# Neighbourhood attention with query tiles shifted by half a key tile, joined context heads, and modulation blocks summed in one op

## The chip, the core and the metric
The kernel runs on one core of a Trainium2 chip. Five engines work from queues of their own: TensorE (PE: matmuls and transposes, with weight loads shown apart as PEld), VectorE (DVE), ScalarE (ACT), GpSimd (POOL) and SyncE (SP), which issues all DMA transfers here. The metric is the device time of one execution in microseconds, as a median of several runs.

## What is computed
One inference step of a backbone of four layers on 128 context tokens and 512 latent tokens (a grid of 8 rows and 64 columns), all in float32. Cut to what matters here:

```
for l in range(4):                      # kind: 0 global, 1 window, 2 neighbourhood, 0 global
    shift, scale, gate = split(silu(c) @ w_mod[l] + b_mod[l])     # for latent and for context
    u = rms_norm(h, norm_pre[l]) * (1 + scale) + shift
    q, k, v, z = split(u @ w_in[l])     # 1024, 256, 256, 1024 columns; q, k get RMSNorm per head
    kind 0, 1: rotary positions on q and k
    latent tokens attend to: kind 0 all latent keys; kind 1 latent keys within +-128;
        kind 2 all 8 rows x a clamped window of 16 columns, with a relative bias per head;
        and always to 128 cached context keys, in one softmax (kind 1 with a sink logit)
    context tokens attend to context tokens only
    h = h + gate * rms_norm((o * silu(z)) @ w_out[l], norm_post[l])
return h_ctx, h_lat, new_cache_k, new_cache_v
```
There are 16 query heads of 64 columns in 4 groups that share keys and values.

## The kernel before
**Order of work.** All instructions are first put down as ops with their reads, writes and buffers (`S.op`, L92). A planner (`emit`, L130) then walks a modelled time and takes, again and again, the op that can start first; ties and look-ahead go by a number for each op, its place in the program plus an offset for the part of the kernel it belongs to (`ORDER`, L29; `MODSHIFT`, `SSHIFT`, `WINDOW`). What it issues on an engine stays in that order on the chip. Buffers are pools with a fixed number of slots (`CAPS` and L227): an op that needs a free slot can't be planned before there is one.

**Precision.** Projections and scores are made of float32r matmuls on a high and a low part of each operand: a copy on ScalarE makes the high part, a subtraction on VectorE (or GpSimd) the low one (`split`, L263). Raw weights come in by tiles of 128x512 (256 KB) into buffers named raw, of which there are six, and are split into buffers named w, of which there are eight (`start_w`, L322).

**A layer.** `kv_chunk` (L561) projects keys and values of five token tiles of 128 (tile 0 is the context). Then, twice, for half of the heads: `q_chunk` (L601) projects, normalizes, rotates and transposes the queries of five tiles into five buffers q, `z_block` (L632) makes the gate, and `lat_pair` (L748) does latent attention for four pairs of heads: scores (L702 for global layers, L728 for the two band layers), the addition of mask or bias with a running maximum (L731), exponential (L741), scaling by the reciprocal sum (L662), transposes of the probabilities (L777) with their eviction (L260), the product with the values (L784) and the product with the gate (L791). `ctx_heads` (L795) does the same for the context's queries in groups of four heads (L804, L830, L838, L843). At the end of a layer `split_og` splits the gated output, and `out_phase` (L910) multiplies by w_out and makes the next layer's input (L455 to L467).

**Layer 2.** Here tokens are ordered by blocks of 16 grid columns, so a key tile is 8 rows x 16 columns and query tiles are the same blocks. A query tile needs its own block and its neighbours, and the context tile (number 4): `BAND` (L45) lists 3, 4, 4 and 3 key tiles for the four query tiles, `UNION` the key tiles of a pair of query tiles, `BATCHES` how their transposes go into PSUM banks (four banks for each half of a pair of heads, with 4, 4, 3 and 3 transposes). `bias_tiles` (L666) builds, for each head, two tiles of bias plus mask on GpSimd from a strided load of the bias table: two clears and four additions, which wait for the last query buffer (L754). The token order is changed in layer 1's last stage (`rows`, L488, and `split_og`), and changed back at the end of layer 2.

**Modulation.** The vector silu(c) for latent and context is multiplied by w_mod in blocks of 512 output columns, as four concurrent column strips of TensorE. A block is two ops of four k each (`mod_half`, L371), which add into one PSUM bank that is held from the first to the second; a half takes four raw buffers, and `cap_raw` lets modulation have no more than four. `mods` (L477) hands out the 40 halves over the phases of the layers by the table `MODS` (L21), so that they fall between other work.

Of the kernel before, what the change touches and what calls it, by code (L numbers as in the profile page):

```python
# [20 lines left out]
MODS = [[1, 3, 3, 3, 2, 0, 0], [1, 3, 3, 3, 2, 0, 0], [1, 3, 3, 3, 2, 0, 0], [1, 2, 1, 0, 0, 0, 0]]  # L21
# [4 lines left out]
           (([(0, (0, 2))], [(1, (0, 2))], [(0, (2, 4))], [(1, (2, 4))]),))  # L26


ORDER = {'mf': -51, 'tab': 230, 'kv': 673, 'ks': -1156, 'nat': 29, 'hn': -564, 'mod': 211, 'w': -2, 'qt': 6,  # L29
         'z': 99, 'sc': 231, 'st': -343, 'pv': -1242, 'cx': 15, 'og': 10, 'out': -36, 'no': 283, 'un': -775,  # L30
         'up': -335, 'bt': -16, '': -11}
MODSHIFT = -121
SSHIFT = -248
WINDOW = 257
# [3 lines left out]
SLACK = {'P': 89, 'V': 0, 'A': 234, 'G': 0, 'D': 521}  # L38
DISLIKE = {'V2': 0, 'V': 933, 'Ap': 365, 'G': 1080, 'mad': 968, 'mada': 3985, 'G1': 612}
CAPS = {'p': 6, 'raw': 6, 'cap_prep': 3}  # L40
# [4 lines left out]
BAND = {0: [0, 1, 4], 1: [0, 1, 4, 2], 2: [1, 2, 4, 3], 3: [4, 2, 3]}  # L45
TILES = ((0, 1), (2, 3, 4))
UNION = {0: [0, 1, 4, 2], 1: [2, 3, 4, 1]}
# [14 lines left out]
class Sched:  # L62
# [17 lines left out]
    def __init__(self, nc):  # L80
        self.nc = nc
        self.eng = {"P": nc.tensor, "V": nc.vector, "A": nc.scalar, "G": nc.gpsimd, "D": nc.sync}
        self.tags, self.ops, self.shift, self.part = {}, [], 0, ""
        self.prev, self.line = [], {}
# [7 lines left out]
    def op(self, alts, r=(), w=(), touch=(), seq=None):  # L92
# [25 lines left out]
        self.ops.append((alts, deps, list(bufs.values()), i + self.shift + ORDER.get(self.part, 0)))  # L118
# [94 lines left out]
def build(ctx, tc, a, o):  # L213
# [61 lines left out]
    identr = persist("identr", [128, 128], F32R)  # L275
    mhalf = persist("mhalf", [128, 1])
    S.op([("G", 1500, lambda e: make_identity(nc, ident.ap), "id")], w=[ident])
    S.op([V2(128, lambda e: e.tensor_copy(identr.ap, ident.ap))], r=[ident], w=[identr])
# [57 lines left out]
    def mod_part(l, b, mod, tag):  # L336
# [15 lines left out]
        S.op([P(935, mm, "E")], r=raws + [cpad], w=[ps], touch=[cap])  # L352
# [18 lines left out]
    def mod_half(l, s, mod, half, st):  # L371
# [7 lines left out]
        for kk, raw in enumerate(raws):  # L379
            S.op([D(256, lambda e, raw=raw, kk=kk: e.dma_start(raw.ap, a["w_mod"][l, s, 4 * half + kk]))], w=[raw],  # L380
                 touch=[caps[kk]])

        def mm(e):
            for kk in range(4):
                k = 4 * half + kk
                for g in range(4):
                    e.matmul(ps.ap[32 * g:32 * g + 32, 0:128], cpad.ap[:, k, :], raws[kk].ap[:, 128 * g:128 * g + 128],  # L387
                             start=k == 0, stop=k == 7, skip_group_check=True)
# [88 lines left out]
    def mods(l, phase, i, n):  # L477
# [3 lines left out]
        for _ in range(m * (i + 1) // n - m * i // n):  # L481
            if queue:
                mod_half(*queue.pop(0))
# [4 lines left out]
    def rows(t, perm, tau):  # L488
        if tau == 0:
            return t[0:128]  # L490
        if perm:
            return t[128:640].rearrange("(r j c) d -> j r c d", r=8, j=4)[tau - 1]
        return t[128 * tau:128 * tau + 128]
# [107 lines left out]
    def q_chunk(l, tabs, c):  # L601
        W = load_w(a["w_in"], l, c)
        Q = []
        for tau in range(5):
            ps, pcap = S.buf("B", [128, 512]), S.buf("cap_proj")
            q = S.buf("q", [128, 8, 128], F32R)
            nat(lambda ps=ps: ps.ap, ps, [pcap], tau, W, [q])
# [13 lines left out]
            for x in range(2):  # L621
                hi, lo = (slice(0, 64), slice(64, 128))[::1 - 2 * x]
                d = lambda rows, x=x, q=q: q.ap.rearrange("p (r x) t -> p x r t", x=2)[rows, x]
                v = lambda hi=hi, pt=pt: pt.ap[hi].rearrange("p (r t) -> p r t", r=4)
                S.op([As(512, lambda e, d=d, v=v, hi=hi: e.activation(d(hi), v(), AF.Copy))], r=[pt], w=[(q, x)], touch=[cap])
                S.op([V(512, lambda e, d=d, v=v, hi=hi, lo=lo: e.tensor_sub(d(lo), v(), d(hi).bitcast(F32)))], r=[pt, (q, x)],  # L626
                     w=[(q, x)], touch=[cap])
            Q.append(q)
# [37 lines left out]
    def bias_tiles(l, h, tabs, after):  # L666
        tab = tabs["tab"]
        raw = lambda: tab.ap[:, 896 + 265 * (h % 2):1161 + 265 * (h % 2)]
        S.op([D(300, lambda e: e.dma_start(raw(), bass.AP(tensor=a["na"].tensor, offset=a["na"].offset + 512 * h,
                                                         ap=[[31, 8], [1, 16], [1, 265]])))], w=[(tab, h % 2)])  # L670

        def rel(a0, n):
            x = raw()
            return bass.AP(tensor=x.tensor, offset=x.offset + 264 - 16 * a0,
                           ap=[list(x.ap[0]), [-16, n], [-31, 8], [-1, 16]])

        b03, b12 = tmp([128, 640]), tmp([128, 512])
        v = lambda x: x.rearrange("p (a r c) -> p a r c", r=8, c=16)
        S.op([G1(128, lambda e: e.memset(b03.ap[:, 256:384], 0.0))], r=after, w=[(b03, 256)])
        S.op([G1(128, lambda e: e.memset(b12.ap[:, 256:384], 0.0))], r=after, w=[(b12, 256)])  # L680
# [398 lines left out]
```

## Time and profile before
| | |
|---|---|
| median of 3 runs | 1366.44 us (1366.27 to 1368.22) |
| the profiled execution | 1366.54 us, of which the span from first to last instruction is 1364.8 us |
| TensorE matmul busy | 1331.3 us (98% of the span) |
| TensorE weight loads busy | 1097.1 us (80%) |
| VectorE, ScalarE, GpSimd busy | 971.9, 753.5 and 212.9 us (71, 55 and 16%) |
| DMA | 145.61 MB, 107 GB/s in the mean |

Busy time of an engine is the union of its instructions. Matmuls are pipelined, so one record is longer than the distance to the next start; what a matmul costs is read from the distances of starts. In a timeline a merged row gives the start of its first instruction, the time to the end of its last, and the count; the distance to the next row's start is what the group took of the engine.

### The profile page before, as it was taken

What the parts mean: (1) busy time and instruction counts of PE and PEld (TensorE: products, weight loads), DVE (VectorE), ACT (ScalarE), POOL (GpSimd) and SP (SyncE); (2) the same over time, 40 slices, a digit from 0 to 9 for tenths busy, and PEclk for the clock granted to TensorE, in tenths of its full rate; (3) what the DMA queues carried; (4) which work ended last, traced back from release to release, by engine and by line L of the source; (5) the groups of instructions that cost most, each with busy time, mean ns of one, the idle gap of its engine ahead of it and who ended that gap; (6) DMA issues with size and microseconds to landing.
All of it is one profiled execution on the core that took longest, in us unless ns stands there. A gap on an engine that the chain in (4) does not pass through costs nothing.

```text
span 1364.8 us, 24827 instructions
## 1 busy us (share of the span) xinstructions
PE 1331.3 (98%) x9208; PEld 1097.1 (80%) x9208; DVE 971.9 (71%) x2298; ACT 753.5 (55%) x1823; POOL 212.9 (16%) x231
## 2 busy tenths in 40 slices
PE   6999999999999999999999999999999999999998
PEld 3778888888877888788878888788777888888876
DVE  4878667766597866876487678678579776586753
ACT  4545663666353675477355368358445366547741
POOL 1320002000142100100032441342023300020000
PEclk9999999999999999999999999999999999999999
DMA  8532222304333423332644343242534220110042
GB/s 339 172 107 80 78 93 81 106 32 161 135 121 96 137 79 93 104 98 72 184 133 135 120 122 102 70 122 67 163 130 155 91 95 1 63 62 1 30 133 101
DMA packets 76521, 145.61 MB, mean 107 GB/s; under 512 B 12976, under 2 KB 17136, under 8 KB 76400
## 3 DMA queue, kind: packets, MB, share of 16 engines
q1 hardware_dynamic: 76400, 144.02, 32.5%
q8 instruction: 73, 1.20, 0.4%
q14 instruction: 48, 0.39, 0.1%
HBM read 132.42 MB, written 11.57 MB: 106 GB/s over the span
## 4 chain that ended last, share of the span: by engine, by line
PE 80%; DVE 13%; issue 3%; ACT 2%; POOL 1%; DMA 1%; SPq 0%; DVEq 0%; POOLq 0%; ACTq 0%
PE B L501 16%; PE B L638 13%; PE B L777 9%; PE B L784 9%; PE S L905 8%; PE B L905 6%; PE S L702 5%; PE S L728 4%; PE B L387 2%; DVE q L626 2%; DVE tmp L467 1%; POOL sm L311 1%; DVE w L266 1%; PE S L501 1%; PE B L618 1%
## 5 line engine op out<-in xcount | busy, mean ns | idle before, releaser
L311 POOL TENSOR_TENSOR sm<-sm,mhalf 128x1 f32<-128x1 f32 (+2 forms) x100 | 130.3, 1305 | 667.6 <-DVE sm L306 352.5
L260 ACT ACTIVATE pt<-B 128x512 f32<-128x512 f32 (+1 forms) x300 | 161.2, 575 | 101.8 <-PE B L777 91.7
L501 PE MATMUL B<-w,uB 128*128 128x512 f32 x816 | 201.3, 399 | 0.0
L501 PEld LDWEIGHTS B<-w,uB 128*128 128x128 f32 x816 | 150.0, 188 | 33.4 <-issue 0.2
L638 PE MATMUL B<-uB,w 128*128 128x384 f32 x768 | 164.6, 345 | 0.0
L777 PE MATMUL B<-ident,p 128*128 128x128 f32 x1088 | 155.1, 277 | 2.1 <-ACT pt L260 0.8
L266 DVE TENSOR_TENSOR w<-raw,w 128x512 fp32r<-128x512 f32 x212 | 141.7, 698 | 5.7 <-ACT w L265 5.2
L777 PEld LDWEIGHTS B<-ident,p 128*128 128x128 f32 x1088 | 122.5, 140 | 24.0 <-issue 8.8
L501 PE MATMUL B<-w,uA 128*128 128x512 f32 x528 | 136.9, 403 | 0.8 <-DVE tmp L467 0.7
L705 DVE TENSOR_REDUCE sm<-S 128x1 f32<-128x640 f32 x128 | 103.5, 821 | 47.6 <-PE S L702 46.7
L265 ACT ACTIVATE w<-raw 128x512 fp32r<-128x512 f32 x224 | 131.7, 626 | 6.6 <-PE B L638 2.8
L784 PE MATMUL B<-pt,vt 128*64 128x256 f32 (+1 forms) x1152 | 131.6, 373 | 0.0
L638 PEld LDWEIGHTS B<-uB,w 128*128 128x128 f32 x768 | 128.6, 189 | 1.5 <-issue 0.7
L662 DVE TENSOR_SCALAR p<-p,sm 128x640 f32<-128x640 f32 (+2 forms) x244 | 123.7, 519 | 6.8
L707 ACT ACTIVATE p<-S,sm 128x640 f32<-128x640 f32 x128 | 101.8, 797 | 42.3 <-DVE sm L705 32.8
L638 PE MATMUL B<-uA,w 128*128 128x256 f32 x768 | 114.7, 286 | 0.1
L501 PEld LDWEIGHTS B<-w,uA 128*128 128x128 f32 x528 | 95.1, 188 | 23.0 <-issue 2.6
L784 PEld LDWEIGHTS B<-pt,vt 128*64 128x64 f32 x1152 | 77.0, 136 | 45.2 <-issue 8.0
L638 PEld LDWEIGHTS B<-uA,w 128*128 128x128 f32 x768 | 102.3, 189 | 2.4 <-issue 0.8
L702 PE MATMUL S<-kst,q 128*128 128x320 f32 x512 | 100.5, 324 | 1.1 <-ACT p L707 0.8
L741 ACT ACTIVATE p<-p,sm 128x512 f32<-128x512 f32 (+1 forms) x128 | 84.0, 658 | 12.0 <-DVE sm L739 11.8
L510 ACT ACTIVATE tmp<-B 128x512 f32<-128x512 f32 (+1 forms) x56 | 30.1, 537 | 106.0 <-PE B L501 82.6
(141 smaller groups left out, 2049.6 us busy)
## 6 DMA issues: line engine op xcount, KB each, us to landing
raw<-in_w_in SPq DMA_DIRECT2D x160, 256.0 KB
raw<-in_w_mod SPq DMA_DIRECT2D x160, 256.0 KB
raw<-in_w_out SPq DMA_DIRECT2D x64, 256.0 KB
w<-in_w_first SPq DMA_DIRECT2D x16, 512.0 KB
xs<-q SPq DMA_DIRECT2D x15, 512.0 KB
q<-xs SPq DMA_DIRECT2D x15, 512.0 KB
q<-in_x SPq DMA_DIRECT2D x10, 512.0 KB
kst<-gs SPq DMA_DIRECT2D x8, 512.0 KB
```

Of the source, the lines that this page charges most:

```text
L260: alts = {"A": Ap(n, lambda e: e.activation(out(), in_(), AF.Copy)), "V": V(n, lambda e: e.tensor_copy(out(), in_()))}
L265: S.op([As(n, lambda e: e.activation(h(), src(), AF.Copy))], r, w)
L266: f = lambda e: e.tensor_sub(l(), src(), h().bitcast(F32))
L311: S.op([("G", 395 + 157 * n, lambda e: e.tensor_tensor(r.ap, v.ap, mhalf.ap.to_broadcast([128, n]), op=OP.pow), "pow")], r=[v, mhalf], w=[r])
L501: e.matmul(ps(), t.ap[:, s, k, off:off + 128], W[k].ap[:, w], start=k == 0 and i == 0, stop=k == 7 and i == 2)
L638: e.matmul(ps.ap[:, 0:w], W[k].ap[:, wi, 128 * f:128 * f + 128], t.ap[:, s, k, :], start=k == 0 and i == 0, stop=k == 7 and i == 2)
L662: f = lambda e, i=i, p=p, w=w: e.tensor_scalar(p.ap[:, 0:w], p.ap[:, 0:w], rs.ap[:, i:i + 1], 1.0, op0=OP.mult, op1=OP.mult)
L702: e.matmul(ps.ap[:, b, 0:320], Q[t + 1].ap[:, hh], kst.ap[:, g, s, 320 * b:320 * b + 320], start=s == 0, stop=s == 1)
L705: S.op([V(640, lambda e, ps=ps, i=i: e.tensor_reduce(negm.ap[:, i:i + 1], ps.ap[:, :, 0:320], axis=AX.XY, op=OP.max, negate=True))], r=[ps ...
L777: e.transpose(pt.ap[:, c:c + 128], p.ap[:, b:b + 128], ident.ap)
L784: e.matmul(po.ap[64 * x:64 * x + 64, 256 * half + q0:256 * half + q0 + w], vt.ap[:, kt, 64 * g:64 * g + 64], sbt.ap[:, c0:c0 + w], start=f ...
L905: e.matmul(ps(), t.ap[:, s, k, off:off + 128], W[k].ap[:, w], start=k == 0 and i == 0, stop=k == 7 and i == 2)
```

## The change
1. **Query tiles of layer 2.** The token blocks are now 8 grid columns wide. A key tile is still two blocks (16 columns), but a latent query tile is the second block of one key tile and the first of the next; the last query tile is the last block and the first one. `BAND` for layer 2 becomes three key tiles for each query tile, `UNION` and `BATCHES` follow (three PSUM banks with four transposes each). The transposed queries of one natural tile are written in halves into two query buffers, so all five buffers are allotted at the start of a chunk. The bias is built as one tile of 512 columns, one of 384 and one in the table buffer, with three additions, two clears (three for the first two heads) and one ScalarE copy; the bias rows come in two transfers of 64 partitions each, as do the permuted rows of layer 1's last stage. The product with the gate is split in 448 and 64 columns.
2. **Context heads.** The two groups of a chunk have one PSUM bank, one op of products with the values, and one product with the gate.
3. **Modulation.** `mod_cols` sums all eight k of a block in one op, from eight raw buffers; there are eight raw buffers instead of six, and `cap_raw` is eight. `MODS` hands out 20 blocks. The unused `identr` is gone.
4. **Planner numbers.** `ORDER` has offsets for each layer; `MODSHIFT`, `SSHIFT`, `WINDOW`, `SLACK` and `DISLIKE` are others.

```diff
-MODS = [[1, 3, 3, 3, 2, 0, 0], [1, 3, 3, 3, 2, 0, 0], [1, 3, 3, 3, 2, 0, 0], [1, 2, 1, 0, 0, 0, 0]]
+MODS = [[0, 1, 2, 1, 2, 0, 0], [0, 1, 2, 1, 2, 0, 0], [0, 1, 2, 1, 2, 0, 0], [0, 1, 1, 0, 0, 0, 0]]
...
-           (([(0, (0, 2))], [(1, (0, 2))], [(0, (2, 4))], [(1, (2, 4))]),))
+           (([(0, (0, 2))], [(1, (0, 2))], [(0, (2, 4))], [(1, (2, 4))]),),
+           (([(0, (0, 2))], [(1, (0, 2))], [(0, (2, 4)), (1, (2, 4))]),))
...
-MODSHIFT = -121
-SSHIFT = -248
-WINDOW = 257
+MODSHIFT = 23
+SSHIFT = -222
+WINDOW = 490
...
-SLACK = {'P': 89, 'V': 0, 'A': 234, 'G': 0, 'D': 521}
+SLACK = {'P': 95, 'V': 0, 'A': 200, 'G': 176, 'D': 1}
...
-CAPS = {'p': 6, 'raw': 6, 'cap_prep': 3}
+CAPS = {'p': 6, 'raw': 8, 'cap_raw': 8, 'cap_prep': 3}
...
-BAND = {0: [0, 1, 4], 1: [0, 1, 4, 2], 2: [1, 2, 4, 3], 3: [4, 2, 3]}
+BAND = {1: {0: [0, 1, 4], 1: [0, 1, 4, 2], 2: [1, 2, 4, 3], 3: [4, 2, 3]},
+        2: {0: [0, 1, 4], 1: [1, 4, 2], 2: [4, 2, 3], 3: [0, 4, 3]}}
+UNION = {1: {0: [0, 1, 4, 2], 1: [2, 3, 4, 1]}, 2: {0: [1, 4, 0, 2], 1: [3, 4, 2, 0]}}
...
-    def mod_half(l, s, mod, half, st):
+    def mod_cols(l, s, mod):
...
-        if half == 0:
-            st[:] = [S.buf("B", [128, 512]), S.buf("cap_mod")]
-        ps, cap = st
-        raws, caps = [S.buf("raw", [128, 512]) for _ in range(4)], [S.buf("cap_raw") for _ in range(4)]
+        ps, cap = S.buf("B", [128, 512]), S.buf("cap_mod")
+        raws, caps = [S.buf("raw", [128, 512]) for _ in range(8)], [S.buf("cap_raw") for _ in range(8)]
...
         def mm(e):
-            for kk in range(4):
-                k = 4 * half + kk
+            for k in range(8):
                 for g in range(4):
...
-        S.op([P(935, mm, "E")], r=raws + [cpad], w=[ps], touch=[cap] + caps)
-        if half == 0:
-            return
+        S.op([P(1920, mm, "E")], r=raws + [cpad], w=[ps], touch=[cap] + caps)
...
-        Q = []
+        Q = [S.buf("q", [128, 8, 128], F32R) for _ in range(5)]
...
+            if tau and KINDS[l] == 2:
+                parts = [(Q[(tau + 2) % 4 + 1], 0, 64, 64, 1), (Q[tau], 64, 0, 64, 0)]
+            else:
+                parts = [(Q[tau], 0, 0, 128, None)]
+            nat(lambda ps=ps: ps.ap, ps, [pcap], tau, W, [x[0] for x in parts])
...
+                    if KINDS[l] == 2:
+                        step = COL[band[1]] - COL[band[0]]
+                        h = lambda s: kst.ap[:, g, s].rearrange("p (a b) -> p a b", b=128)[:, COL[band[0]]:COL[band[2]] + 1:step]
+                        parts = [(0, w, h)]
...
+        for a0, b0, w in ((0, 64, 448), (448, 0, 64)) if KINDS[l] == 2 else ((0, 0, 512),):
+            gt = lambda b0=b0, w=w: gate.ap[:, pr, 128 + b0:128 + b0 + w]
...
-            S.op([P(505, mv, "C")], r=[sbt, (vt, VC)], w=[po], touch=[ocap])
+        S.op([P(1090, mv, "C")], r=tiles + [(vt, VC)], w=[po], touch=[ocap])
```

## Rows read from the trace of the kernel before

**Rows 1.** The page's busy times of the engines (us, share of the span, instructions), and the granted clock of TensorE in 40 equal slices of the span, in tenths of full speed (9 is 90% or more).
```profile
PE 1331.3 (98%) x9208; PEld 1097.1 (80%) x9208; DVE 971.9 (71%) x2298; ACT 753.5 (55%) x1823; POOL 212.9 (16%) x231
...
PEclk9999999999999999999999999999999999999999
```

**Rows 2.** The list of waits of TensorE over the whole span, 18 rows of which these are the first two and two from the middle: line that waited, what it waited for, us in total, times, longest.
```profile
PE B L350 <- DMA raw<-in_w_in: 10.9, 1, 10.9
PE B L618 <- DVE tmp L532: 5.1, 10, 0.7
...
PE B L777 <- ACT pt L260: 0.8, 3, 0.5
...
PE B L387 <- PE S L702: 0.4, 2, 0.2
```

**Rows 3.** Busy time by engine (PE, PEld, DVE, ACT, POOL, with instruction counts), granted clock, DMA share and GB/s in the four windows of layer 2: keys, values and first query projections; first four pairs of heads; second query projections; second four pairs.
```profile
702.00:768.00 66.00, 65.51 (x358) 51.90 (x358) 48.84 (x107) 30.56 (x68) 18.65 (x14) 1.00 0.40 125
768.00:846.00 78.00, 77.42 (x692) 66.15 (x691) 59.26 (x180) 51.06 (x124) 27.51 (x51) 1.00 0.40 121
846.00:880.00 34.00, 34.00 (x204) 27.17 (x204) 19.60 (x39) 15.49 (x41) 7.33 (x5) 1.00 0.17 57
880.00:958.00 78.00, 77.36 (x667) 66.32 (x665) 64.69 (x194) 52.88 (x138) 27.25 (x51) 1.00 0.36 105
```

**Rows 4.** TensorE's timeline, from several stretches: start us, us to the end of the row's last instruction, line, shape, count.
```profile
197.74 0.66 PE L838 MATMUL B<-pt,vt 128*64 128x128 f32 x8
198.33 1.08 PE L387 MATMUL B<-raw,cpad 128*32 128x128 f32 x32
199.34 0.66 PE L830 MATMUL B<-ident,p 128*128 128x128 f32 x4
...
778.54 1.08 PE L387 MATMUL B<-raw,cpad 128*32 128x128 f32 x32
...
779.78 1.81 PE L638 MATMUL B<-uA,w 128*128 128x256 f32 x14
781.43 3.29 PE L638 MATMUL B<-uB,w 128*128 128x384 f32 x18
...
786.41 0.87 PE L638 MATMUL B<-uA,w 128*128 128x256 f32 x6
787.22 1.08 PE L387 MATMUL B<-raw,cpad 128*32 128x128 f32 x32
...
795.67 1.74 PE L784 MATMUL B<-pt,vt 128*64 128x256 f32 x16
797.33 1.08 PE L387 MATMUL B<-raw,cpad 128*32 128x128 f32 x32
...
1241.76 2.38 PE L784 MATMUL B<-pt,vt 128*64 128x256 f32 x20
1244.07 2.49 PE L777 MATMUL B<-ident,p 128*128 128x128 f32 x20
...
1314.64 4.36 PE L905 MATMUL S<-w,uB 128*128 128x512 f32 x18
```

**Rows 5.** Groups of TensorE's instructions by line and shape in layer 2 (702 to 958 us): count, busy us, mean ns of one record, idle before.
```profile
L638 PE MATMUL B<-uB,w 128*128 128x384 f32 x192 | 41.4, 346 | 0.0
...
L777 PE MATMUL B<-ident,p 128*128 128x128 f32 x224 | 33.4, 277 | 0.5 <-ACT pt L260 0.2
...
L784 PE MATMUL B<-pt,vt 128*64 128x256 f32 x192 | 24.2, 388 | 0.0
...
L728 PE MATMUL S<-kst,q 128*128 128x384 f32 x64 | 17.0, 354 | 0.0
...
L728 PE MATMUL S<-kst,q 128*128 128x256 f32 x64 | 11.2, 297 | 0.0
L728 PE MATMUL S<-kst,q 128*128 128x512 f32 x32 | 10.2, 400 | 0.0
...
L784 PE MATMUL B<-pt,vt 128*64 128x128 f32 x64 | 6.2, 273 | 0.0
```

**Rows 6.** The same view, groups of VectorE and ScalarE: the query copies of layer 2, and the nearest copies of half their columns.
```profile
L626 DVE TENSOR_TENSOR q<-B,q 64x512 fp32r<-64x512 f32 x20 | 13.8, 689 | 10.4 <-ACT q L625 10.1
...
L625 ACT ACTIVATE q<-B 64x512 fp32r<-64x512 f32 x20 | 11.8, 592 | 15.7 <-PE B L618 15.5
...
L555 DVE TENSOR_TENSOR kst<-B,kst 128x256 fp32r<-128x256 f32 x12 | 4.8, 421 | 3.6 <-ACT kst L554 3.6
...
L554 ACT ACTIVATE kst<-B 128x256 fp32r<-128x256 f32 x12 | 4.3, 382 | 2.6 <-PE B L550 2.3
```

**Rows 7.** From the list of waits of SyncE's queue over the whole span (us in total, times, longest), and from the timeline around the first pairs of heads of layer 2: transfers issued, the gate's matmuls, and the addition on GpSimd with its idle time before and what ended it.
```profile
SPq L326 <- PE B L387: 165.2, 21, 20.5
...
738.29 1.26 SPq L326 DMA_DIRECT2D raw<-in_w_in  x2
...
762.17 3.80 SPq L326 DMA_DIRECT2D raw<-in_w_in  x6
...
769.16 0.88 PE L638 MATMUL B<-uA,w 128*128 128x256 f32 x6
...
780.23 1.27 SPq L669 DMA_DIRECT2D tab<-in_na  x2
...
785.18 1.54 POOL L682 TENSOR_TENSOR tmp<-tab 128x256 f32<-128x256 f32 x2 [6.08 <-DMA tab<-in_na]
```

More of the change, by code (lines that the diff above doesn't have):

```diff
@@ L117, in op @@
             b.ops += 1
-        self.ops.append((alts, deps, list(bufs.values()), i + self.shift + ORDER.get(self.part, 0)))
+        self.ops.append((alts, deps, list(bufs.values()), i + self.shift + ORDER.get(self.part + str(self.layer), ORDER.get(self.part, 0))))
     def named(self, part):
@@ L482, in mods @@
             if queue:
-                mod_half(*queue.pop(0))
+                mod_cols(*queue.pop(0))
         S.shift = old
@@ L488, in rows, with move_rows, f @@
     def rows(t, perm, tau):
[L489 to L493, printed above, removed]
+        if tau and perm:
+            f = t[128:640].rearrange("(r j c) d -> j r c d", r=8, j=8)
+            return [(slice(64 * y, 64 * y + 64), f[2 * tau - 2 + y]) for y in range(2)]
+        return [(slice(0, 128), t[128 * tau:128 * tau + 128])]
+    def move_rows(x, t, perm, tau, out=False):
+        def f(e):
+            for ps, r in rows(t(), perm, tau):
+                e.dma_start(*((r, x.ap[ps]) if out else (x.ap[ps], r)))
+        return D(512, f)
     @S.named("nat")
@@ L622, in q_chunk @@
                 hi, lo = (slice(0, 64), slice(64, 128))[::1 - 2 * x]
[L623 to L628, printed above, removed]
+                for q, a0, b0, w, part in parts:
+                    d = lambda rows, x=x, q=q, b0=b0, w=w: q.ap.rearrange("p (r x) t -> p x r t", x=2)[rows, x, :, b0:b0 + w]
+                    v = lambda hi=hi, pt=pt, a0=a0, w=w: pt.ap[hi].rearrange("p (r t) -> p r t", r=4)[:, :, a0:a0 + w]
+                    keys = [(q, (x, y)) for y in (range(2) if part is None else [part])]
+                    S.op([("A", 3.333 * w + 185, lambda e, d=d, v=v, hi=hi: e.activation(d(hi), v(), AF.Copy), "As")], r=[pt],
+                         w=keys, touch=[cap])
+                    S.op([("V", 4.167 * w + 175, lambda e, d=d, v=v, hi=hi, lo=lo: e.tensor_sub(d(lo), v(), d(hi).bitcast(F32)),
+                           "V")], r=[pt] + keys, w=keys, touch=[cap])
         return Q
@@ new lines, in bias_tiles @@
+        if h < 2:
+            S.op([G1(128, lambda e: e.memset(wrap()[:, 128:256], 0.0))], r=after, w=[(tab, (x, "z"))])
+        for dst, key, m0, n, a0 in ((lambda: b02.ap[:, 128:384], (b02, 128), 0, 2, 0),
+                                    (lambda: wrap()[:, 0:128], (tab, (x, "w", 1)), 256, 1, 1),
+                                    (lambda: wrap()[:, 256:384], (tab, (x, "w", 0)), 384, 1, 0)):
+            f = lambda e, dst=dst, m0=m0, n=n, a0=a0: e.tensor_tensor(v(dst()), v(tab.ap[:, m0:m0 + 128 * n]), rel(a0, n), op=OP.add)
+            S.op([G(128 * n, f)], r=rd, w=[key])
@@ L688, in scores @@
+        S.op([Ap(256, lambda e: e.activation(tiles(b1.ap)[:, 0:3:2], tiles(b02.ap)[:, 1:3], AF.Copy))], r=[(b02, 128)], w=[(b1, 0)])
+        return {0: ([b02], lambda: b02.ap[:, 128:512]), 1: ([b1], lambda: b1.ap), 2: ([b02], lambda: b02.ap[:, 0:384]),
+                3: ([(tab, (x, k)) for k in ("z",)] + [(tab, (x, "w", k)) for k in range(2)], wrap)}
     @S.named("sc")
@@ L761, in lat_pair @@
             else:
-                where = {kt: [(i, BAND[2 * half + i].index(kt)) for i in range(2) if kt in BAND[2 * half + i]] for kt in UNION[half]}
-                batches = BATCHES[1]
+                band, union = [BAND[KINDS[l]][2 * half + i] for i in range(2)], UNION[KINDS[l]][half]
+                where = {kt: [(i, band[i].index(kt)) for i in range(2) if kt in band[i]] for kt in union}
+                batches = BATCHES[KINDS[l]]
             for n, batch in enumerate(batches):
@@ L768, in lat_pair @@
                     for x, part in tile:
-                        for kt in (UNION[half] if KINDS[l] else range(5))[part[0]:part[1]]:
+                        for kt in (union if KINDS[l] else range(5))[part[0]:part[1]]:
                             at.setdefault(kt, []).append((x, sbt, c, 128 * len(where[kt]), 128 * where[kt][0][0]))
@@ L941, in out_phase @@
             j = min(tau, 1)
-            S.op([D(512, lambda e, x=x, tau=tau: e.dma_start(x.ap, rows(xin(), order(l), tau)))], r=xdep + [(ysc, first[tau])], w=[x])
+            S.op([move_rows(x, xin, order(l), tau)], r=xdep + [(ysc, first[tau])], w=[x])
             ps, cap = S.buf("B", [128, 512]), S.buf("cap_out")
@@ L962, in out_phase @@
             else:
-                S.op([D(512, lambda e, x=x, tau=tau: e.dma_start(rows(xdst.ap, order(l), tau), x.ap))], r=[x], w=[(xdst, tau)])
+                S.op([move_rows(x, lambda: xdst.ap, order(l), tau, True)], r=[x], w=[(xdst, tau)])
                 u_phase(tau, x, mod[l + 1][1])
@@ L991, in build @@
     for l in range(DEPTH):
-        for s in range(0 if l else 4, 6):
-            st = []
-            queue += [(l, s, mod[l], half, st) for half in range(2)]
+        queue += [(l, s, mod[l]) for s in range(0 if l else 4, 6)]
     for l in range(DEPTH):
+        S.layer = l
         tabs = tables(l)
```

111 lines of the change are left out of this document (52 added, 59 removed), and 9 rows, old and new, of the table ORDER.

## The prediction, made before the changed kernel was run
> **What bounds the kernel now.** I read the page's totals and slices first, then the list of what TensorE waited for, then the stages, and last the spacing of matmuls in the timeline. The reader is to see four things. TensorE's matmul row is busy for 1331.3 of 1364.8 us, and the granted clock is full in every slice [rows 1]. One wait of 10.9 us is the very start, where the first weights come in; the other 17 rows of the list add up to 13.8 us, of which 5.1 are transposes of queries and keys that wait for VectorE's rotation (L618) [rows 2]. In the four windows of layer 2 no other engine is at its limit: VectorE is busy 48.8, 59.3, 19.6 and 64.7 us of 66, 78, 34 and 78 [rows 3]. And within a run of equal matmuls the starts follow at a pace set by the columns: 18 of 512 columns span 4.36 us with the last record's 0.40, so 17 steps of 233 ns; 18 of 384 span 3.29 with 0.35, steps of 173 ns [rows 4, 5]. Both are 2.2 columns a nanosecond, a little under the 2.4 GHz level. So a matmul that is removed gives its time back, unless a wait takes its place.
>
> One rule of the Trainium skill speaks against this reading: "Perfetto Trace Analysis", section "Identifying the Most-Contended Engine", says that matmul busy time is no good measure of how near TensorE is to its limit, and wants the busy share of the weight loads. That share is 80% here, against 98% [rows 1]. By the rule a fifth of the engine might be free, and removed work might only leave gaps; by the pace of the rows it does not. This is rival D below.
>
> **Part 1, layer 2's neighbourhood attention.** A query tile shifted by half a key tile needs two key tiles and the context, so the four bands are 3+3+3+3 tiles of 128 keys instead of 3+4+4+3: 12 for 14, in each of 16 heads.
> - Scores (L728). Before: 64 matmuls of 384 columns, 64 of 256 and 32 of 512 [rows 5], at 0.173, 0.118 (14 of them take 779.78 to 781.43) and 0.233 us [rows 4]: 11.1 + 7.5 + 7.5 = 26.1 us. After: 8 of 384 per head, 128 x 0.173 = 22.1 us. Saved 4.0 us.
> - Transposes of probabilities (L777). 224 become 192 [rows 5]. Twenty span 2.49 us with the last record's 0.28 [rows 4, 5]; 0.10 of the rest is the cost of leaving the group before (part 2), so a step is 0.11: saved 3.5 us.
> - Probabilities times values (L784). 192 records of 256 columns and 64 of 128, in 16 groups [rows 5]. A group has 12 and 4 and takes 1.66 us (795.67 to 797.33), where layer 3's group of 20 wide ones takes 2.31 us [rows 4]. Records go in concurrent pairs, so with p for a wide pair, p/2 for a narrow one and c fixed, 10p + c = 2.31 and 7p + c = 1.66: p = 0.217. After, a group has 4 wide and 4 narrow pairs, 6p + c: 0.22 us less, times 16: saved 3.5 us.
>
> Together 11.0 us of TensorE. What the part adds lies on other engines, and I cost it at nothing.
> - The query copies. Each of eight latent query tiles (two chunks of four) is copied in halves into two buffers: four ScalarE and four VectorE copies of 64x256 for two of 64x512 each. No row has this shape; the nearest are 128x256 copies at 0.382 and 0.421 us, against 0.592 and 0.689 now [rows 6], so +0.34 and +0.31 us a tile. From below, two halves cost no less than the whole (0); from above, each costs a full copy (+1.2 and +1.4 us). I take the nearest: 2.8 and 2.4 us in all, in windows where ScalarE is busy 30.6 of 66 and 15.5 of 34 us [rows 3]. What hides the last tile's copies is the gate's matmuls (L638), which TensorE runs without a pause after the chunk's last projections, from 779.78 to past 784 in the first one [rows 4].
> - Scores of tile 0 now wait for natural tiles 1 and 2, those of tile 3 for 4 and 1. But the bias waited for the last query buffer already (L754), and without a bias no score leaves its PSUM bank (L731), so the start of the softmax moves by no more than the copies above.
> - The bias is three additions instead of four, of 512 columns instead of 896, plus one ScalarE copy of 256 columns (0.38 us by the same nearest row), on a GpSimd that is busy 27.5 of 78 us [rows 3]. Exponentials, sums, scalings and evictions all lose two of 14 tiles, and the evictions of half a pair of heads are three instead of four. The product with the gate is in two pieces, eight times, one fixed cost more each.
> - Two-part transfers (16 heads of bias, four tiles each way in layer 1) add 24 issues to a SyncE queue that waits for buffers most of the time.
>
> If this cover failed, the price is the extra 0.7 us of copies and about 0.5 us of bias chain at the head of each of the two chunks, 2 to 3 us.
>
> **Part 2, modulation in one op.** Each of 20 blocks is now 64 records in a row instead of twice 32. A half takes 1.01 us from its first start to the next instruction's (198.33 to 199.34); 0.81 of that is its 31 intervals (1.08 less a record's 0.27), 0.113 for each step of four [rows 4]. Joined: 1.01 + 8 x 0.113 = 1.91 for 2.02, saved 0.11 us. Besides, going into such a group costs its neighbour: six matmuls of 256 columns took 0.81 us before one (786.41 to 787.22), 0.71 by their pace [rows 4], so 0.10 us once less where the neighbour isn't itself a group in column strips. 20 x 0.11 to 20 x 0.21 is 2.2 to 4.2 us; both kinds of neighbour stand in the rows, so I take the middle, 3.2. And the PSUM bank of a sum is no longer held from one half to the next, 8.7 us in one case (778.54 to 787.22 [rows 4]).
>
> **Part 3, joined context heads.** 16 groups of 8 records (0.59 us each, 197.74 to 198.33) become 8 of 16. Three intervals span 0.39 us (0.66 less 0.27) [rows 4], so 0.59 + 4 x 0.13 = 1.11 for 1.18, or with 0.11 a step 1.03; with 0.10 for one entry, 0.17 to 0.25 us saved, times 8: 1.3 to 2.0, I take 1.6. VectorE has eight products of 512 columns for sixteen of 256.
>
> **Part 4, the order.** New offsets per layer, a longer look-ahead and other slacks reorder everything. No row prices this. The bounds are the waits: the 13.8 us could go entirely, or as much could be added. A free PSUM bank and fewer evictions bear on waits such as L777's for an eviction (0.8) and L387's behind the scores (0.4) [rows 2], about 2 us in all; these I take as gained, and nothing else.
>
> **The sum.** 4.0 + 3.5 + 3.5 + 3.2 + 1.6 + 2.0 = 17.8 us. The profiled execution took 1366.54 us (span 1364.8), 0.1 from the median 1366.44. 1366.4 - 17.8 = 1348.6 us. The bounds of parts 2 and 3 and a quarter of the waits either way give 1344 to 1353.
>
> **Rivals.**
> B, the new order also removes most remaining waits, 8 to 10 us more: 1340. For it: the wait at L618 comes ten times [rows 2], and offsets per layer can treat these stages separately. Against: each is the end of a chain through four engines.
> C, layer 2 stays bound by its chain of bias, sum, exponential, scaling, transpose and eviction; half of part 1 is lost, and 3 us come at the heads of the chunks: 1348.6 + 5.5 + 3 = 1357. For it: VectorE is busy 64.7 of 78 us in the last such window [rows 3], which would shrink to some 72.5. Against: TensorE idles for 0.6 us of that window [rows 3].
> D, TensorE's busy time is no bound and the gaps stay: within 0.2% of 1366. The even pace speaks against it [rows 4].
> E, slower: a block keeps all eight raw buffers until its product, so the next chunk's weights can't be requested before it. The mechanism is in the trace: the queue waited 165.2 us, 21 times, at weight loads for a modulation product. In layer 2 two weights went ahead at 738.29, six followed at 762.17, after a product, and the gate's matmuls began at 769.16. A transfer took about 4.9 us until its reader went on (780.23 to 785.18) [rows 7], and two splits, at the price of the query copies, 0.59 + 0.69 [rows 6]: 6.2 us, so the cover was about 1 us, with two of the buffers free of modulation, which none is now. It decides from the point where the product comes less than 6.2 us before the last projection matmul of a stage. 14 blocks stand there (in seven chunks one at the last query tile and one at the last pair of heads); each 2 us late, they add 28 us: 1376.
>
> **How the numbers follow.** Forecast 0.62, B 0.15, C 0.11, D 0.04, E 0.08. Faster by over 0.2%, about what a measurement of this kernel can tell from no change: 0.62 + 0.15 + 0.11 = 0.88; the same 0.04; slower 0.08. The range 1340 to 1358 takes in the forecast, C and half of B, and leaves out about 0.19.
>
> **What would show it.** L728 with 128 matmuls of 384 columns in layer 2 and none of 512 there; L777 and L784 shorter by 3.5 us each; 20 runs of 64 modulation records near 1.9 us; waits of TensorE below 13 us beside the start. Wrong would be: waits of TensorE on weight splits or raw transfers (E), waits at L777 or L728 in layer 2 above 3 us (C), or matmul spacing stretched without a wait (D).

## The result, and the profile after

| | before | after |
|---|---|---|
| median, us | 1367.33 (1366.27 to 1368.86) | 1335.82 (1335.39 to 1338.66) |
| profiled execution, us (span) | 1366.54 (1364.8) | 1338.66 (1336.8) |

The ratio is 0.9773, 95% interval 0.9755 to 0.9791: 31.5 us faster, where 17.8 were forecast, and 4 us below the lower end of the range. The page's totals and the granted clock, beside [rows 1]:

```profile
PE 1309.4 (98%) x9144; PEld 1097.7 (82%) x9144; DVE 853.8 (64%) x2058; ACT 745.8 (56%) x1839; POOL 388.4 (29%) x472
...
PEclk9999999999999999999999999999999999999999
```
TensorE is as full as before. The slices of the clock look as before, but they are 33 us wide and hide one short stretch at half, shown below. What catches the eye is that 118 us have left VectorE and 175 have come to GpSimd; part 1 of the prediction had them both lighter. The group that moved is the scaling of the probabilities, of which 244 were on VectorE and 12 on GpSimd (the first two lines, of before). Now all are on GpSimd (groups of instructions by line):

```profile
L662 DVE TENSOR_SCALAR p<-p,sm 128x640 f32<-128x640 f32 (+2 forms) x244 | 123.7, 519 | 6.8
L662 POOL TENSOR_SCALAR p<-p,sm 128x640 f32<-128x640 f32 (+2 forms) x12 | 8.7, 724 | 210.1 <-DVE sm L661 129.6 <-DVE sm L658 77.2 <-PE B L387 2.5
...
L676 POOL TENSOR_SCALAR p<-p,sm 128x640 f32<-128x640 f32 (+2 forms) x256 | 185.3, 733 | 337.4 <-DVE sm L675 235.9 <-DVE sm L672 38.0 <-PE B L392 14.8
```

The list of TensorE's waits, beside [rows 2] (18 rows; this one has 11, of which the first six):

```profile
PE B L359 <- DVE cpad L298: 6.6, 1, 6.6
PE B L458 <- DVE q L437: 3.8, 3, 1.9
PE B L392 <- DMA raw<-in_w_mod: 2.6, 3, 2.1
PE B L630 <- DVE tmp L547: 1.4, 3, 0.6
PE B L652 <- DVE w L277: 1.2, 2, 0.6
PE S L757 <- DVE q L641: 1.1, 2, 0.6
```
The first wait is shorter by 4.3 us. The ten waits of query transposes for the rotation (5.1 us) are gone; L630 is what was L618, and what is left there are three waits in layer 2, which has no rotation; before there were two such, 0.6 us. L652's two waits are on weight splits in layer 3; before, no matmul of the gate waited for a split. The third row is one place, at 671.5 us.

Layer 2 by groups (675 to 935 us, beside [rows 5, 6]):

```profile
L676 POOL TENSOR_SCALAR p<-p,sm 128x384 f32<-128x384 f32 x64 | 37.7, 603 | 35.8 <-DVE sm L675 32.2 <-DVE sm L768 1.7 <-DVE gate L822 0.9
L757 PE MATMUL S<-kst,q 128*128 128x384 f32 x128 | 28.1, 352 | 1.1 <-DVE q L641 1.1
...
L807 PE MATMUL B<-ident,p 128*128 128x128 f32 x192 | 26.2, 273 | 0.1
...
L814 PE MATMUL B<-pt,vt 128*64 128x256 f32 x128 | 17.3, 392 | 0.0
...
L641 DVE TENSOR_TENSOR q<-B,q 64x256 fp32r<-64x256 f32 x32 | 12.8, 420 | 9.7 <-ACT q L639 6.4 <-PE B L510 3.0
L639 ACT ACTIVATE q<-B 64x256 fp32r<-64x256 f32 x32 | 10.7, 374 | 14.8 <-PE B L630 9.3 <-DVE q L641 5.2
...
L814 PE MATMUL B<-pt,vt 128*64 128x128 f32 x128 | 9.7, 273 | 0.0
```
128 score matmuls of 384 columns, 192 transposes, and 128 + 128 records of the product: the counts of part 1. The half copies take 0.420 and 0.374 us, where the nearest rows had given 0.421 and 0.382.

TensorE's timeline there, beside [rows 4]:

```profile
782.29 1.52 PE L814 MATMUL B<-pt,vt 128*64 128x256 f32 x16
783.75 1.66 PE L757 MATMUL S<-kst,q 128*128 128x384 f32 x8
...
790.56 1.96 PE L392 MATMUL B<-raw,cpad 128*32 128x128 f32 x64
792.44 1.67 PE L757 MATMUL S<-kst,q 128*128 128x384 f32 x8
```
A group of products takes 1.46 us (1.66 less 0.22 was said), a joined block of modulation 1.88 (1.91 was said).

And the place of the one long wait on a transfer, which shows rival E in small: a block begins, and the sixth of its eight raw tiles has not landed. Behind the timeline stands a row of the view of windows, with the same columns as [rows 3]; the seventh is the granted clock.

```profile
668.15 1.30 PE L392 MATMUL B<-raw,cpad 128*32 128x128 f32 x40
671.53 0.42 PE L392 MATMUL B<-raw,cpad 128*32 128x128 f32 x8 [2.08 <-DMA raw<-in_w_mod]
...
673.94 1.63 PE L940 MATMUL B<-w,uB 128*128 128x512 f32 x3
675.37 0.41 PE L397 MATMUL B<-ident,pm 128*128 128x128 f32 x1
```
```profile
673.30:676.70 3.40, 3.40 (x11) 2.81 (x12) 1.97 (x7) 2.12 (x6) 0.55 (x1) 0.50 0.64 201
```
Right behind the wait the granted clock is 0.50, the 1.2 GHz level, until 676.7 us. Three matmuls of 512 columns take 1.43 us there, 0.48 each for 0.232 elsewhere, and the stretch costs 1.5 us beyond the pace. Both costs belong to this execution: the profiled one took 2.8 us more than the median, and in experiments e5 and e7 below, whose queues have the same order, the same line waits 0.2 and 0.5 us and the clock is full from 22 us on until the last matmuls are done.

**The balance.** The distance from each TensorE record's start to the next one's, summed over the profiled execution, can be sorted completely. Plain matmuls and transposes count at the pace of their columns (232, 174.5, 147, 118 and 109 ns for 512, 384, 320, 256 and 128), groups in column strips count whole, "entry" is what goes beyond the pace before such a group, "waits" is what goes beyond it before a record that the profile shows as idle for over 20 ns.

```
us                                      before          after    difference
to the first matmul                       10.9            6.6       -4.3
plain matmuls and transposes, at pace   1099.7         1092.4       -7.3
products with values (L784, L814)        127.2          124.0       -3.2
modulation (L387, L392)                   41.8           40.9       -0.9   (2.6 of it the wait at 671.5)
first modulation (L350, L359)             11.7           11.3       -0.4
context products (L838, L873)              9.4            8.2       -1.2
entry into column strips           9.9 for 105     8.1 for 86       -1.8
waits                              21.9 for 50    14.3 for 25       -7.6
the rest, small stretches                 25.1           23.9       -1.2
after the last start                       7.1            7.1        0.0
span                                    1364.8         1336.8      -28.0
```
Three groups of modulation before run straight into a wait of the next line, 1.4 us in all (1.48, 1.46 and 1.48 for 1.01). In "the rest" after, 1.5 us are the stretch at half clock. So the work removed is 7.3 + 3.2 + (0.9 + 2.6 - 1.4) + 1.2 + 1.8 = 15.6 us, against 15.8 in parts 1 to 3. What was not foreseen is the remainder of some 15 us: waits 7.6 + 1.4, start 4.3, the two small rows 1.6.

The start's 4.3 us are not kept. The first 36.5 us of plain matmuls are done at 64.7 us before and at 63.7 after, so 1.1 us are left there: the transposes of L458 wait for 3.8 us (1.87, 1.59 and 0.37), and all waits up to this point cost 5.6 us for 2.4. From there on the waits cost 8.7 us (21) for 19.5 (47). So 12 us of the remainder, with the 1.4 in modulation, are waits that are gone after the first 64 us.

### The profile page after: what moved, and what is told of

Same layout as the page of the kernel before. It is cut to its first block, busy times and chain, and to the rows that moved or that the text cites. A ratio compares the mean times of both kernels' runs of the same rounds, so it can differ in the third digit from the quotient of the medians.

```text
span 1336.8 us, 24963 instructions
## 1 busy us (share of the span) xinstructions
PE 1309.4 (98%) x9144; PEld 1097.7 (82%) x9144; DVE 853.8 (64%) x2058; ACT 745.8 (56%) x1839; POOL 388.4 (29%) x472
## 4 chain that ended last, share of the span: by engine, by line
PE 91%; DVE 3%; ACT 2%; issue 2%; DMA 1%; POOL 0%; DVEq 0%; SPq 0%; POOLq 0%; ACTq 0%
PE B L510 22%; PE B L652 15%; PE B L814 9%; PE B L807 9%; PE S L940 8%; PE B L940 8%; PE S L726 6%; PE S L757 4%; PE B L392 3%; PE S L510 2%; PE B L458 1%; PE B L630 1%; PE S L836 1%; DVE q L641 1%; PE B L559 1%
## 5 line engine op out<-in xcount | busy, mean ns | idle before, releaser
L676 POOL TENSOR_SCALAR p<-p,sm 128x640 f32<-128x640 f32 (+2 forms) x256 | 185.3, 733 | 337.4 <-DVE sm L675 235.9
L271 ACT ACTIVATE pt<-B 128x512 f32<-128x512 f32 (+1 forms) x273 | 149.5, 585 | 84.5 <-PE B L807 77.2
L652 PE MATMUL B<-uB,w 128*128 128x384 f32 x768 | 163.1, 344 | 0.0
L807 PE MATMUL B<-ident,p 128*128 128x128 f32 x1056 | 144.5, 274 | 0.1
L652 PEld LDWEIGHTS B<-uB,w 128*128 128x128 f32 x768 | 129.3, 188 | 1.8 <-issue 1.3
L814 PE MATMUL B<-pt,vt 128*64 128x256 f32 (+1 forms) x1152 | 128.2, 367 | 0.0
L652 PE MATMUL B<-uA,w 128*128 128x256 f32 x768 | 115.5, 286 | 1.2 <-DVE w L277 1.2
L652 PEld LDWEIGHTS B<-uA,w 128*128 128x128 f32 x768 | 103.4, 188 | 3.1 <-DVE w L277 1.6
L770 ACT ACTIVATE p<-p,sm 128x384 f32<-128x384 f32 (+1 forms) x128 | 80.5, 631 | 10.0 <-DVE sm L768 9.9
L726 PEld LDWEIGHTS S<-kst,q 128*128 128x128 f32 x512 | 77.9, 189 | 6.5 <-issue 1.9
```

The costliest lines, as they stand in the source:

```text
L271: alts = {"A": Ap(n, lambda e: e.activation(out(), in_(), AF.Copy)), "V": V(n, lambda e: e.tensor_copy(out(), in_()))}
L652: e.matmul(ps.ap[:, 0:w], W[k].ap[:, wi, 128 * f:128 * f + 128], t.ap[:, s, k, :], start=k == 0 and i == 0, stop=k == 7 and i == 2)
L676: f = lambda e, i=i, p=p, w=w: e.tensor_scalar(p.ap[:, 0:w], p.ap[:, 0:w], rs.ap[:, i:i + 1], 1.0, op0=OP.mult, op1=OP.mult)
L726: e.matmul(ps.ap[:, b, 0:320], Q[t + 1].ap[:, hh], kst.ap[:, g, s, 320 * b:320 * b + 320], start=s == 0, stop=s == 1)
L807: e.transpose(pt.ap[:, c:c + 128], p.ap[:, b:b + 128], ident.ap)
L814: e.matmul(po.ap[64 * x:64 * x + 64, 256 * half + q0:256 * half + q0 + w], vt.ap[:, kt, 64 * g:64 * g + 64], sbt.ap[:, c0:c0 + w], start=f ...
```

## The experiments

Three kinds of kernels: parts exchanged and everything planned anew (e1 to e4); edits that keep every queue in the order that the planner gave (e5 to e8); and one planner number moved a little (e9 to e18). Ratios are to the kernel before, run beside each on the same chip; the changed kernel's is 0.9773.

**e1 to e4: exchange a part, and plan anew.**

```diff
 # e1: the changed kernel with before's numbers (e3: DISLIKE alone)
-ORDER = {'0': -27, 'mf0': -44, ...}; MODSHIFT = 23; SSHIFT = -222; WINDOW = 490; ...
+ORDER = {'mf': -51, 'tab': 230, ...}; MODSHIFT = -121; SSHIFT = -248; WINDOW = 257; ...
 # e2: the kernel before with the changed kernel's numbers
+S.layer = l      # and ORDER looked up with the layer
 # e4: the changed kernel with modulation as before
-queue += [(l, s, mod[l]) for s in range(0 if l else 4, 6)]
+queue += [(l, s, mod[l], half, st) for half in range(2)]      # mod_half, raw: 6, cap_raw: 4, MODS of before
```

> The changed kernel with the planner numbers of before (one offset per part, old shifts, window, slacks and dislikes). Theory N (the numbers): the structural edits give the 16 us that the prediction summed without its part 4, the rest of the 31 us comes from the numbers, so about 1351 us (1347 to 1355). Theory S (the structure): shorter bands, one free PSUM bank and fewer evictions also remove waits, and bring nearly all of it, so 1340 us or less.

> The kernel before with the planner numbers of the changed one, and nothing else of it. Theory N: about 15 us less than before, 1352 us (1348 to 1357). Theory S: the numbers alone do nothing or harm, 1363 us or more.

> The changed kernel with only the planner's dislikes of before, by which the scaling of the probabilities goes back from GpSimd to VectorE (V2 0 instead of 2029). If the free VectorE is what took the waits away, 1341 us or more, with waits of transposes for VectorE back in the list. If it was the offsets and the look-ahead, 1336 to 1338 us.

> The changed kernel with modulation undone: blocks in two halves of four k, six raw buffers, four of them for modulation. The prediction's term: 3.2 us more than the changed kernel, 1339 us; with the held PSUM bank costing waits as well, up to 1342. Rival: eight raw buffers help the weights too, more than 1343.

| | median, us | ratio (95%) | waits of TensorE (count) | the rest |
|---|---|---|---|---|
| e1, new parts, old numbers | 1370.96 | 1.0021 (1.0012 to 1.0030) | 37.3 (61) | 31.4 |
| e2, old parts, new numbers | 1408.96 | 1.0303 (1.0289 to 1.0316) | 53.1 (67) | 37.4 |
| e3, old dislikes only | 1366.55 | 0.9995 (0.9984 to 1.0006) | 33.6 (45) | 32.9 |
| e4, modulation in halves | 1376.47 | 1.0067 (1.0055 to 1.0079) | 40.1 (60) | 31.3 |

In e1 both theories fell: it lies above N's range and S's. In e2 N fell; S's 1363 us or more came true, by harm. e3 lies on the side of the free VectorE (1341 or more) and e4 on that of its rival (more than 1343), but all four are new plans, so they price no part. The removed work is there in e1 (1092.4 us of plain matmuls, 123.8 of products, as in the changed kernel), but against the kernel before its waits cost 15 us more and the rest 6 more. What e1's TensorE waits for is spread over all stages (list of its waits):

```profile
PE S L750 <- DVE sm L753: 3.1, 5, 2.0
PE S L719 <- ACT p L724: 3.1, 4, 1.2
PE B L552 <- DVE tmp L463: 2.8, 2, 2.0
```
Part of that rest is the clock. Before the last matmuls are done, the granted clock falls to half in three stretches in e1, six in e2, three in e3 and two in e4, and in none of the kernel before. Each lies beside a single idle time of TensorE of 1.2 to 3.5 us, and the plain matmuls in them take 5.5, 8.7, 5.2 and 3.2 us beyond their pace.

e1 and e2 also say something of the ten waits for the rotation, L618 <- L532 in the kernel before. In e1 (old numbers, new parts) they would be L623 <- L534, and its list has none; the one row of L623 is layer 2's. In e2 (new numbers, old parts) they are L625 <- L539 (lists of waits of e1 and e2):

```profile
PE B L623 <- DVE tmp L540: 1.2, 2, 0.9
```
```profile
PE B L625 <- DVE tmp L539: 5.9, 8, 1.2
```
Of the other runs, those with the old parts have 7 to 10 such waits, those with the new ones none to 4. So these waits went with the parts, not with the offsets per layer; which line of the parts did it was not tested.

These numbers and parts fit only each other. And undoing a part this way doesn't price the part: e4 is 40 us slower for a term of 3.2, because it is a new plan that nobody chose.

**e5 and e6: the scalings on the other engine, same order.** The planner decides as before, and the instruction is issued on another engine at the same place in the sequence.

```diff
-            fn(self.eng[e])
+            fn(self.eng['V' if e == 'G' and getattr(fn, 'scaling', False) else e])     # e6: 'G' for 'V'
...
+            f.scaling = True
             S.op([G1(w, f), V2(w, f)], r=[p, rs if KINDS[l] == 1 else (rs, i)], w=[p])
```

> The changed kernel with every queue in the same order, but the 256 scalings of probabilities issued on VectorE in place of GpSimd (at the same place in the sequence). If it is the load taken off VectorE that removed waits, the time goes up by 5 us or more (1341 to 1360). If the order alone did it, 1335 to 1338 us, since VectorE would be busy 71% again, as before.

> The kernel before with every queue in the same order, but its 244 scalings on VectorE issued on GpSimd. If VectorE's load causes waits there, 1360 us or less. If not, 1366 to 1370 us, more if GpSimd's 0.73 us for 0.52 us shows on the way to a transpose.

e5 took 1341.99 us, 0.9820 (0.9806 to 0.9833): 6.2 us more than the changed kernel, some 3 either way by the two intervals, as expected if the load is what counts. Its waits cost 19.1 us (35) for 14.3 (25). The transposes (L808) have a wait behind VectorE that the changed kernel's list doesn't have, and the gate's matmuls (L652) wait four times for weights where there were two:

```profile
PE B L808 <- DVE gate L660: 1.9, 3, 0.6
PE B L652 <- DVE w L277: 1.6, 4, 0.6
```
e6 took 1376.86 us, 1.0073 (1.0060 to 1.0087), 10 us more than the kernel before: the transposes now wait for GpSimd, whose scaling of 640 columns takes about 0.8 us for VectorE's 0.55 (list of waits of e6; groups by shape, before and e6).

```profile
PE B L778 <- POOL p L662: 4.9, 19, 0.5
```
```profile
L662 DVE TENSOR_SCALAR p<-p,sm 128x640 f32<-128x640 f32 x122 | 67.4, 552 | 4.5
```
```profile
L662 POOL TENSOR_SCALAR p<-p,sm 128x640 f32<-128x640 f32 x128 | 106.2, 832 | 205.2 <-DVE sm L661 203.3 <-PE B L778 1.1
```
So the lighter VectorE is worth about 6 us in an order that is planned around it, and the longer scaling costs 10 in one that isn't. Both lie off TensorE; in the balance they show mostly as waits (4.8 us in e5, 7.6 in e6).

**e7: the work put back, same order.** In layer 2 the changed kernel repeats a 128-column score tile for one of the four query tiles of a head (two matmuls), two transposes for each half of a pair of heads, and a narrow product for each head and half, where a later instruction writes the same or the final value. The planner doesn't know of them.

```diff
-                        parts = [(0, w, h)]
+                        parts = [(0, w, h)] + ([(256, 128, lambda s: h(s)[:, 2:3])] if t == 1 else [])
...
-                        for c, p, b in mv:
+                        for c, p, b in mv + mv[:1] * more:          # more: layer 2, two tiles of three
...
+                            if KINDS[l] == 2 and first and m == 0:
+                                e.matmul(po.ap[64 * x:64 * x + 64, 256 * half + q0:256 * half + q0 + 128],
+                                         vt.ap[:, kt, 64 * g:64 * g + 64], sbt.ap[:, c0:c0 + 128], start=True, stop=False,
+                                         skip_group_check=True)
```

> The changed kernel in the same order, with the work that part 1 took from TensorE put back as repeats whose result is overwritten or equal: in layer 2 one more score tile per head, two more transposes and one narrow product per half pair and head. If removed matmuls give their time back one to one, 11 us more: 1345 to 1348 us. If layer 2 waited for other engines anyway (rival C), 1341 us or less.

1346.44 us, 0.9850 (0.9837 to 0.9864): 10.6 us more than the changed kernel, some 3 either way by the two intervals, for 11.0 in part 1's sum. In the balance the plain matmuls are up by 7.0 and the products by 3.5 (123.3 + 4.3 for 124.0), 10.5 together, and the waits stay (13.7 for 24). The profiled executions differ by only 5.9 us, since the changed kernel's has the late transfer and the stretch at half clock, 2.2 and 1.5 us that e7's has not. By the medians, removed matmuls give their time back one to one; rivals C and D are out.

**e8: the start.** VectorE's queue at the start of the kernel before, and of the changed one (timelines):

```profile
10.42 0.17 DVE L301 TENSOR_SCALAR sink<-sink 128x16 f32<-128x16 f32 x1 [8.79 <-DMA sink<-in_sink]
10.50 0.17 DVE L288 TENSOR_SCALAR th<-th 128x16 f32<-128x16 f32 x1
10.71 0.17 DVE L289 TENSOR_TENSOR cpad<-th,cnd 128x16 f32<-128x16 f32 x1
```
```profile
6.14 0.17 DVE L297 TENSOR_SCALAR th<-th 128x16 f32<-128x16 f32 x1 [4.64 <-ACT th L295]
6.35 0.18 DVE L298 TENSOR_TENSOR cpad<-th,cnd 128x16 f32<-128x16 f32 x1
...
10.21 0.16 DVE L310 TENSOR_SCALAR sink<-sink 128x16 f32<-128x16 f32 x1
```
The first matmul needs cpad. Before, a small product that nobody needs before layer 1 stood ahead of it and waited for its own transfer. [rows 2] name the load of raw weights as the releaser, since it came last by the profile; e8 shows that it was this queue, since the first matmul moves with cpad. e8 only issues L301's op after cpad.

> The kernel before in the same order, except that VectorE's small product of the sink logits, which waits for a late transfer at the head of its queue, is issued just after the padded conditioning vector instead of just before it. If this wait is why the first matmul started at 10.9 us instead of 6.6, the first matmul starts 2 to 4 us earlier; if nothing else bounds the start, the whole is 2 to 4 us shorter, 1363 to 1366 us. If the first weights bound the start, no change in the total.

```profile
8.77 0.17 DVE L293 TENSOR_SCALAR th<-th 128x16 f32<-128x16 f32 x1 [7.14 <-ACT th L291]
8.98 0.17 DVE L294 TENSOR_TENSOR cpad<-th,cnd 128x16 f32<-128x16 f32 x1
```
The first matmul starts at 9.2 us, and 1366.57 us remain, ratio 0.9997 (0.9988 to 1.0006): 1.7 us gained at the head are lost in the next stretches (the rest is 26.9 for 25.1). The rest of the way to 6.6 is the conditioning vector's load, which is the third transfer in the changed kernel and the fifth before. So of the 4.3 us at the start it is open how much reaches the end; 3.7 us are left at the first projection (21.6 and 17.9 us) and 1.1 in the first query projections (64.7 and 63.7); in e8 nothing is left there (64.9).

**e9 to e18: neighbours.** One number moved by ten, everything planned anew.

```diff
-MODSHIFT = 23            # e9: 33, e13: 13; before: -121, e10: -111, e14: -131
-SSHIFT = -222            # e11: -212, e15: -232; before: -248, e12: -238, e16: -258
-SLACK = {'P': 95, ...}   # e17: 105; before: 89, e18: 99
```

> The changed kernel with one planner number moved a little (MODSHIFT 33 for 23). If its waits are low because this order was picked out among many, a neighbour costs 8 us or more (1344 to 1365). If low waits belong to this structure and this kind of numbers, 1334 to 1339 us.

> The kernel before with the same number moved by the same step (MODSHIFT -111 for -121). If its order was picked out too, 1375 to 1395 us. If not, 1364 to 1370 us.

> The changed kernel with the offset of the scores moved a little (SSHIFT -212 for -222). As for the other shift: 1344 to 1365 us if the order was picked out, 1334 to 1339 us if not.

> The kernel before with the same step (SSHIFT -238 for -248): 1375 to 1395 us if its order was picked out, 1364 to 1370 us if not. If the neighbours of both lie equally far above them, the distance between the neighbours is the worth of the structure and the kind of numbers, and the prediction's 15.8 us should be found in it.

> The changed kernel with MODSHIFT 13 for 23. If the changed kernel is a picked order of a cloud whose middle lies 12 us above it: 1342 to 1354 us. If the first two neighbours were bad draws: 1334 to 1340.

> The kernel before with MODSHIFT -131 for -121. If its cloud lies as high above it as that of the changed kernel: 1372 to 1386 us. If the kernel before was no better than its neighbours: 1364 to 1370.

> The changed kernel with SSHIFT -232 for -222: as the run before, 1342 to 1354 us in a cloud, 1334 to 1340 if not.

> The kernel before with SSHIFT -258 for -248: 1372 to 1386 us in a cloud as high as the other, 1364 to 1370 if not.

> The changed kernel with TensorE's slack 105 for 95: 1342 to 1354 us if it is a picked order in a cloud, 1334 to 1340 if not.

> The kernel before with TensorE's slack 99 for 89: 1372 to 1386 us in a cloud as high as the other, 1364 to 1370 if not.

| | MODSHIFT +10 | -10 | SSHIFT +10 | -10 | slack +10 | mean | the kernel itself |
|---|---|---|---|---|---|---|---|
| changed, us | 1348.14 | 1351.31 | 1347.99 | 1337.29 | 1337.94 | 1344.5 | 1335.82 |
| ratio | 0.9861 | 0.9891 | 0.9863 | 0.9780 | 0.9787 | | 0.9773 |
| before, us | 1384.67 | 1369.76 | 1368.14 | 1372.60 | 1378.25 | 1374.7 | 1367.33 |
| ratio | 1.0127 | 1.0024 | 1.0012 | 1.0040 | 1.0080 | | 1 |

Both kernels lie below all five of their neighbours, by 9 and 7 us in the mean, though e12, e15 and e17 by only 1 to 2 us, which the intervals hardly tell apart: each is an order picked among many, to about the same degree. Six of the ten fell where a picked order was expected, e12, e14, e15 and e17 where not. The neighbours are 30 us apart in the mean (25 by their medians, 1347.99 and 1372.60), much more than the 15.6 of the work. So the extra gain is not only a pick of these three numbers: also beside it, this structure with these offsets waits less. But all five neighbours share the long list of offsets in `ORDER`, and whether that list is itself a luckier pick on one side was not tested. In the balance the neighbours' waits are 14.7 to 23.3 us on the changed side and 21.4 to 35.5 on the other.

## Why the prediction was wrong

- **What bounds the kernel**: right. TensorE's time at pace, put back, comes back at the end one to one (e7). One reading was off: the 17 rows of waits beside the start add up to 14.6 us, not 13.8. The weight-load rule of "Perfetto Trace Analysis", section "Identifying the Most-Contended Engine", in the Trainium skill (rival D) doesn't hold here as a sign of free time: the weight loads' share is 82% after, and work put back still cost its full time.
- **Part 1**: right within half a microsecond on TensorE, 10.5 us by the balance (7.3 + 3.2) and 10.6 by e7, for 11.0. The cover, costed at nothing, held only in part. The half copies cost what the nearest rows said, but at the heads of layer 2's two chunks TensorE idles for 2.5 us (three waits at L630, two at L757 for a query copy) where it idled for 1.1 before (0.6 and 0.5); that falls among the waits of part 4.
- **Parts 2 and 3**: right within a microsecond, 5.1 us for 4.8. A block takes 1.9 us in the mean for 2.02, the context products 8.2 for 9.4 in all, and 19 entries fewer save 1.8 us, 94 ns each. The Trainium skill's "TensorEngine Tiling (Array Packing)", section "Key Properties", says that a change of tiling mode drains TensorE; the trace agrees, with these 94 ns at each entry. That the three parts together come within 0.2 us of their sum is luck in part, since the misses of part 1 and of parts 2 and 3 have opposite signs.
- **Part 4**: this is the step that failed, by size. "These I take as gained, and nothing else" took 2 us; beyond the work removed, some 15 us went: in the balance 9 in waits, 4.3 at the start (of which 1.1 outlast the first 64 us, the others come back as waits there), the remainder in small stretches. Three things were missed. First, the move of the scalings could have been read, though not its price: `DISLIKE` puts 2029 on a VectorE scaling where there had been 0, and the scalings are one group of 124 us on VectorE; e5 prices it at 6 us. Second, the parts themselves took waits away: the ten for the rotation (5.1 us of idle time) go with the parts (e1, e2), and the sum gave them to no part. Third, I counted the waits by their idle time, and the list after still adds up to 13.4 us beside the start (with 2.6 of the one late transfer) for 14.6. But 50 waits became 25, and each costs more than its idle time (below).
- **Rival B** came nearest, and its bound of 8 to 10 us was too small, since it left out the cost of a wait beyond its gap. The ten waits for the rotation are gone, as it said, but its reason, offsets per layer, is not what the runs show: without such offsets the waits are gone too (e1), and with them in the kernel before eight remain (e2).
- **Rivals C and E**: C is out by e7. E shows at one place, 2.1 us of wait and 1.5 of half clock in one execution, and perhaps in the gate's two waits on weight splits, 1.2 us, whose cause was not followed up; its cover elsewhere was enough.

What stays open: how the gain beyond the work divides between the parts' own effect on waits, the offsets per layer, the look-ahead and the free PSUM bank. e5's 6 us and the ten waits may overlap, so they can't be added. Every edit to one of them is a new plan, and the new plan after a step of one number alone moves the time by 1 to 17 us.

## What to carry to other kernels

Where one engine is full, sum the removed instructions at the spacing of their starts; that sum was right to half a microsecond in each part. Price a re-planned order as a term of its own, with a range taken from what a small step of one number does, which here is up to 17 us, as much as all the work removed; and read each planner number for the instructions that it moves to another engine. To price a part of a change in a planned kernel, keep the queues' order and put the work back (e7), instead of undoing the part and planning anew (e4: 40 us for a term of 3.2).

## What the runs showed of the hardware

- A wait costs TensorE more than the idle time that the profile shows: 50 waits with 13.5 us of gaps took 21.9 us beyond the pace, 25 with 10.0 took 14.3, so 0.17 us each on top. That is by how much a record is longer than the distance of starts: 0.273 us for 0.109 at 128 columns, 0.352 for 0.1745 at 384, 0.40 for 0.232 at 512. The idle time shown begins only at the record's end.
- A long wait can cost more than its time, since the clock falls beside it. Of the 28 single idle times of TensorE over 1.2 us after the start, in all twenty profiled executions, 21 have a stretch at a granted clock of 0.5 (the 1.2 GHz level) that begins in them or within 4 us behind them; between the start and the last matmuls only one more such stretch stands, behind an idle time of 1.1 us. In the changed kernel's, from 673.3 to 676.7 us, it cost 1.5 us beyond the wait of 2.1. The runs show the two side by side, not what makes the clock fall.
- A chain of small in-order instructions at the start decides the first matmul: one op of 0.17 us, ahead in VectorE's queue and waiting there for its own transfer, held it for some 1.7 us, though without effect on the end.
